# The first two feed-forward tiles of a streaming encoder step by plain products, the seven-product form from the third on

## The chip, the cores and the metric

The kernel runs on one core of a Trainium2 chip. The metric is the time of one launch in microseconds (us) of the device; lower is better. PE is the matrix engine, DVE the vector engine, ACT the scalar engine, POOL the general engine, SP the queue that issues most of the DMAs.

## What is computed

One inference step of a one-layer encoder for 1024 prompt tokens and 8 x 16 sample tokens, 1152 in all, width 1024. The part that matters here is the passage from the first sub-layer to the gated MLP:

```python
x = x + rmsnorm(merged @ p['w_out'], p['g_post1'])
h2 = rmsnorm(x, p['g_pre2'])
...
up = h @ w_ffn_up                      # h = h2: 1152 x 1024 by 1024 x 5632
a, g = jnp.split(up, 2, axis=-1)       # 2816 columns each
ext = jnp.concatenate([buf.astype(a.dtype), a], axis=1)
conv = ext[:, 0:L] * w_dw[0]
for k in range(1, CONV_W):
    conv = conv + ext[:, k:k + L] * w_dw[k]
act = jax.nn.gelu(conv + b_dw) * g
return act @ w_ffn_down
```

## The kernel before

The tokens are held in three chunks of 384 columns (0, 1, 2), features on the partitions in eight blocks of 128. Every matrix product of float32 values is made of three: each operand is split into a high part (ACT copies it to the rounded type, line 63) and a low part (DVE subtracts, line 64), and `mm3` (lines 103, 106, 107) adds hi·hi, hi·lo and lo·hi into one bank of PSUM. Four banks are called `pc`, four `ps`.

`phase_o` multiplies by `w_out`: for chunk c = 0, 1, 2 and output block f = 0 to 7, `out(c, f)` is 24 matmuls of 128x384. ACT copies the bank to `merged[c]` (`mg0`, `mg1`, `mg2` in the traces) and squares it. For each chunk there follow two chains. In the first, `sums` (line 1072) adds the squares over the partitions on PE, `rsqrt` makes the row factors, `row_bcast` (line 96) spreads them over the partitions by one more PE instruction, and `resid` on DVE scales the eight blocks (line 1102), adds x (line 1106; x is loaded and the sum stored to `Dx2` by SP) and accumulates the squares of the result in `ssa` (line 1064). In the second, `sums` and `row_bcast` come again and `norm` (line 1124) scales the rows in place: h2. The chains of chunk c - 1 run beside the products of chunk c; those of chunk 2 run beside the first products of the up GEMM.

The up GEMM works on 22 tiles of ff. Tile ff has two weights of 1024 x 128, one for `a` and one for `g`, which `up_raw` loads into the ring `raw` of three buffers of 512 KB. For chunks 0 and 1 it uses a form with seven products in place of eight: `a` and `g` are the two block rows, the lower and upper four blocks of the inner dimension the two block columns, chunks 0 and 1 the two columns of the right side. The right side's operands are made once: B11, B21 (chunk 0, lower and upper blocks), B22 and T1 to T4 (sums and differences of chunks 0 and 1); those of the left side for each tile by `up_w`: S1 to S4, from the raw weights. Each is split. `up_prod` is one of the seven products: 12 matmuls, then an addition on DVE (or ACT and POOL). Chunk 2 is done by `up_last`, 24 matmuls for `a` and 24 for `g`, with the split weights themselves. `up_act` makes the convolution and the GELU, `up_out` multiplies by `g` and stores.

For tiles 0 and 1 the order is written out at the end of `phase_o`: products 1 and 2 of tile 0, the sums of chunk 2, products 6 and 5, the residual of chunk 2, and so on; the tail of chunk 2 is interleaved. At the start of `phase_u` the weights of these two tiles are loaded and split a second time for chunk 2. From tile 2 on a loop prepares tile ff + 1 while tile ff is multiplied.

The scheduler orders each engine's instructions by a timeline of its own, except where `keep_in_program_order`, `high_priority` or `issue_after` bind it. Each engine, and SP's queue, runs its own list in that order. The pools are rings: `w1` has six tiles of split weights, `w2` four, `m` nine large ones.

Of the kernel before, what the change touches and what calls it, by code (L numbers as in the profile page):

```python
# [10 lines left out]
AF = mybir.ActivationFunctionType  # L11
# [21 lines left out]
class K:  # L33
# [26 lines left out]

    def split(self, hi, lo, src, eng=None):
        nc = self.nc
        nc.scalar.activation(hi, src, AF.Copy)  # L63
        (eng or nc.vector).tensor_sub(lo, src, hi)  # L64

    def load_raw(self, src, shape=(128, 8, 128)):
        r = self.rawtile(list(shape))
# [962 lines left out]
    def phase_o(self):  # L1030
        nc, tc = self.nc, self.tc
        V, G = nc.vector, nc.gpsimd
# [4 lines left out]
        if True:  # L1037
# [75 lines left out]
            def norm(c, rs):  # L1113

                oT = self.merged[c]
                rb = self.row_bcast(P, rs, 3, pin=True)
                if c == 2:
                    self.hhi2 = self.mtile([128, 8, 384], F32R, "h2hi")
                    self.hlo2 = []
                    for tag, n in (("x", 2), ("x", 2), ("ssa", 1), ("ssa", 1), ("sq", 1), ("tmp", 1)):  # L1120
                        t = P.tile([128, n, 384], F32R, tag=tag, name="h2lo")
                        self.hlo2 += [t[:, i] for i in range(n)]
                for f in range(8):
                    V.scalar_tensor_tensor(oT[:, f, :], oT[:, f, :], self.vec[:, V_GPRE2 + f:V_GPRE2 + f + 1], rb,  # L1124
                                           op0=OP.mult, op1=OP.mult)
                    if c == 2:
                        self.split(self.hhi2[:, f, :], self.hlo2[f], oT[:, f, :])

            def op(name, src, eng=None):
                t = self.mtile([128, 2, 4, 384], F32R, "b" + name)  # L1130
# [2 lines left out]

            ss = []
            NF = (0, 5, 4)
            self.B = {}
            lo, up = slice(0, 4), slice(4, 8)
            h0, h1 = self.merged[0], self.merged[1]
            for c in range(3):
                ss.append(ssa())  # L1140
                for f in range(8):
                    self.pin_sq = c == 2
                    if c == 2 and f == 2:
                        self.raws = {0: self.up_raw(0)}
                    out(c, f)
                    if c:
                        if f == 0:
                            rs = sums(ss[c - 1])
                        elif f == 1:
                            with tc.high_priority():  # L1150
                                ss2 = resid(c - 1, rs)
                        elif f == NF[c]:
                            rs = sums(ss2)
                        elif f == NF[c] + 1:
                            with tc.high_priority():
                                norm(c - 1, rs)
                            if c == 1:
                                op("B11", h0[:, lo])
                                op("B21", h0[:, up])
                                V.tensor_sub(h0[:, up], h0[:, up], h0[:, lo])  # L1160
            wms.close()
            self.open_u()
            s0 = self.up_begin(0)
            self.up_w(s0)

            op("B22", h1[:, up])
            V.tensor_sub(h0[:, lo], h1[:, lo], h0[:, lo])
            V.tensor_sub(h1[:, lo], h1[:, up], h1[:, lo])
            V.tensor_sub(h1[:, up], h1[:, up], h0[:, lo])
            op("T2", h1[:, up])  # L1170
            op("T1", h0[:, lo])
            V.tensor_sub(h0[:, up], h0[:, up], h1[:, lo])
            op("T3", h1[:, lo])
            op("T4", h0[:, up])
            self.raws[1] = self.up_raw(1)
            s1 = self.up_begin(1)

            def prods(s, *ps):
                for p in ps:
                    self.up_prod(s, p)  # L1180

            prods(s0, 1, 2)
            rs = sums(ss[2])
            prods(s0, 6, 5)
            with tc.high_priority():
                ss2 = resid(2, rs)
            with tc.issue_after(self.diag.ins):
                self.up_w(s1)
            prods(s0, 7, 3, 4)
            prods(s1, 1, 2)  # L1190
            rs = sums(ss2)
            prods(s1, 6, 5)
            norm(2, rs)
            prods(s1, 7, 3, 4)
            self.first = s0, s1


    def open_u(self):
# [21 lines left out]

    def up_w(self, s, eng=(None,) * 4):

        G = self.nc.vector if s.ff < 2 else self.nc.gpsimd
        ra, rg = self.raws[s.ff]
        a11, a12, a21, a22 = ra[:, 0:4], ra[:, 4:8], rg[:, 0:4], rg[:, 4:8]
        s.aw = self.load_w(None, pool=self.w2, r=ra)
# [11 lines left out]
        s1, s2 = stage()  # L1238
# [15 lines left out]
    def up_prod(self, s, p):  # L1254
# [2 lines left out]
        V = nc.vector  # L1257
        an, bn = {1: ("A11", "B11"), 2: ("A12", "B21"), 6: ("S2", "T2"), 5: ("S1", "T1"), 7: ("S3", "T3"),
                  3: ("S4", "B22"), 4: ("A22", "T4")}[p]
        b = (self.pc() if s.ff < 2 else self.sm())[:, 0:384]  # L1260
        (ah, al), (bh, bl) = s.A[an], self.B[bn]
        for k in range(4):
            self.mm3(b, ah[:, k, :], al[:, k, :], bh[:, k, :], bl[:, k, :], k == 0, k == 3, k == 0)
# [51 lines left out]

    def phase_u(self):
        for s in self.first:

            self.raws[s.ff] = self.up_raw(s.ff)
            s.aw = self.load_w(None, pool=self.w2, r=self.raws[s.ff][0])  # L1320
            self.up_last(s, "a")
            self.up_act(s)
            self.up_wg(s)
            self.up_last(s, "g")
            self.up_out(s)
        cur = None
# [517 lines left out]
```

## Time and profile before

| | us |
|---|---|
| median of 3 runs | 1606.23 (1605.18 to 1611.32) |
| profiled execution | 1607.13 |
| its span in the trace | 1605.3 |
| PE busy | 1546.5 (96%) |
| DVE busy | 1044.1 (65%) |
| ACT busy | 586.4 (37%) |
| mean granted clock of PE | 0.98 |

How to read it: a row of the timeline gives the start in us from the span's start, the time in us, the engine, the line, the operation and its tiles (out<-in), the number of instructions in the row, and in brackets how long the engine was idle before it and what released it. Instructions overlap in the pipe: the starts of a row and of the next give the pace, the durations a little more. A row of the windows gives the length of a stretch, then for each engine its busy time and number of instructions, the granted clock of PE (1.00 is full), the share of the DMA engines and GB/s.

### The profile page before, as it was taken

To read this page: it belongs to the slowest core of one execution; us is meant where nothing else is said; L and a number is where in the kernel's file an instruction comes from. 1 tells how busy PE (TensorE), PEld (TensorE's weight loads), DVE (VectorE), ACT (ScalarE), POOL (GpSimd) and SP (SyncE) were. 2 spreads that over 40 slices of the span, in tenths; PEclk is the share of its full clock that TensorE was granted. 3 is DMA by queue.
4 is the path that set the end of the run, shared out by engine and by line. 5 is a ranking of instruction groups with operands and counts; after the bars stand their busy time and mean duration, and the time that the engine had idled before them with its cause. 6 is when DMAs were issued, how large, how long until landed. Compare 5 with 4: busy or idle time off the path is not lost.

```text
span 1605.3 us, 22914 instructions
## 1 busy us (share of the span) xinstructions
PE 1546.5 (96%) x8964; PEld 1512.9 (94%) x8964; DVE 1044.1 (65%) x1602; ACT 586.4 (37%) x894; POOL 510.8 (32%) x460
## 2 busy tenths in 40 slices
PE   6899999999999999999889999999999999999996
PEld 5899999789899999999879999999999998999996
DVE  7873997655743354637777565656565658788866
ACT  6322544442421242435435433333333333333321
POOL 2400001100021143300016435443443326655546
PEclk9899999999999999999789999999999999999998
DMA  6343333434332235122323211221212143133214
GB/s 247 98 150 96 101 110 107 162 106 117 105 120 81 67 84 164 54 91 91 114 89 138 82 69 66 72 82 69 76 62 82 70 136 137 48 101 105 89 65 167
DMA packets 98460, 163.44 MB, mean 102 GB/s; under 512 B 23216, under 2 KB 68656, under 8 KB 98352
## 3 DMA queue, kind: packets, MB, share of 16 engines
q1 hardware_dynamic: 97920, 161.75, 30.5%
q8 instruction: 70, 1.15, 0.3%
q14 instruction: 38, 0.31, 0.1%
q10 hardware_dynamic: 432, 0.23, 0.0%
HBM read 119.52 MB, written 42.42 MB: 101 GB/s over the span
## 4 chain that ended last, share of the span: by engine, by line
PE 80%; DVE 9%; DMA 3%; issue 2%; ACT 2%; POOL 1%; POOLq 0%; SPq 0%; DVEq 0%; ACTq 0%
PE pc L107 15%; PE pc L103 15%; PE pc L106 14%; PE ps L103 11%; PE ps L106 11%; PE ps L107 11%; DMA Ts<-DG 1%; PE ps L849 1%; DMA DG<-gs 1%; DVE wlo L64 1%; DVE Xs L598 1%; PE ps L1072 1%; DVE mg L1124 1%; PE ps L763 0%; DVE sg L200 0%
## 5 line engine op out<-in xcount | busy, mean ns | idle before, releaser
L103 PE MATMUL pc<-hhi,whi 128*128 128x384 f32 x760 | 259.1, 341 | 7.3 <-ACT hhi L126 7.3
L106 PE MATMUL pc<-hlo,whi 128*128 128x384 f32 x760 | 258.4, 340 | 2.7 <-DVE hlo L127 2.7
L107 PE MATMUL pc<-hhi,wlo 128*128 128x384 f32 x760 | 257.9, 340 | 0.3 <-DVE wlo L64 0.3
L63 ACT ACTIVATE whi<-rawt 128x1024 fp32r<-128x1024 f32 x102 | 107.5, 1055 | 188.6 <-PE pc L106 83.4
L64 DVE TENSOR_TENSOR wlo<-rawt,whi 128x1024 fp32r<-128x1024 f32 x102 | 128.5, 1262 | 56.2 <-ACT whi L63 55.8
L103 PEld LDWEIGHTS pc<-hhi,whi 128*128 128x128 f32 x760 | 144.6, 190 | 9.8 <-ACT hhi L126 7.3
L106 PEld LDWEIGHTS pc<-hlo,whi 128*128 128x128 f32 x760 | 144.2, 190 | 5.4 <-DVE hlo L127 3.6
L107 PEld LDWEIGHTS pc<-hhi,wlo 128*128 128x128 f32 x760 | 144.3, 190 | 2.3 <-issue 0.7
L200 DVE TENSOR_TENSOR sg<-pc,rb 128x384 f32<-128x384 f32 x95 | 52.3, 553 | 117.8 <-PE pc L107 117.4
L107 PE MATMUL pc<-h2hi,wlo 128*128 128x384 f32 x352 | 119.1, 338 | 2.1 <-DVE wlo L64 2.0
L103 PE MATMUL pc<-h2hi,whi 128*128 128x384 f32 x352 | 118.3, 336 | 0.0
L106 PE MATMUL pc<-h2lo,whi 128*128 128x384 f32 x352 | 118.2, 336 | 0.0
L63 ACT ACTIVATE S<-S 128x512 fp32r<-128x512 f32 x88 | 55.3, 630 | 157.9 <-PE ps L107 89.8
L64 DVE TENSOR_TENSOR S<-S,S 128x512 fp32r<-128x512 f32 x88 | 72.5, 826 | 56.2 <-ACT S L63 54.2
L924 ACT ACTIVATE sg<-sg,vec 128x384 f32<-128x384 f32 x72 | 44.1, 613 | 139.0 <-DVE sg L200 108.3
L1011 POOL TENSOR_TENSOR mg<-mg,sgl 128x384 f32<-128x384 f32 x24 | 29.1, 1212 | 165.4 <-DVE sgl L1009 162.0
L103 PE MATMUL ps<-bT,S 128*128 128x384 f32 x240 | 80.2, 334 | 0.0
L107 PE MATMUL ps<-bT,S 128*128 128x384 f32 x240 | 80.2, 334 | 0.0
L106 PE MATMUL ps<-bT,S 128*128 128x384 f32 x240 | 80.2, 334 | 0.0
L63 ACT ACTIVATE dhi<-dwr 128x1024 fp32r<-128x1024 f32 x38 | 39.7, 1058 | 95.2 <-PE pc L106 60.7
L107 PEld LDWEIGHTS pc<-h2hi,wlo 128*128 128x128 f32 x352 | 66.1, 188 | 2.8 <-DVE wlo L64 2.8
L1244 POOL TENSOR_TENSOR S<-rawt 128x512 f32<-128x512 f32 x20 | 27.2, 1361 | 125.6 <-PE ps L107 125.6
(463 smaller groups left out, 4349.7 us busy)
## 6 DMA issues: line engine op xcount, KB each, us to landing
rawt<-in_w_up SPq DMA_DIRECT2D x48, 512.0 KB, 3.4
Dact<-t SPq DMA_DIRECT2D x22, 576.0 KB, 3.5
rawt<-in_w_gate SPq DMA_DIRECT2D x24, 512.0 KB, 3.6
dwr<-in_w_down SPq DMA_DIRECT2D x22, 512.0 KB, 3.4
Dsg<-sg SPq DMA_DIRECT2D x45, 192.0 KB, 1.9
sgl<-Dsg SPq DMA_DIRECT2D x45, 192.0 KB, 2.4
dBr<-Dact SPq DMA_DIRECT2D x8, 768.0 KB, 5.7
xT<-in_xT SPq DMA_DIRECT2D x12, 384.0 KB, 7.6
```

The lines of the kernel that those rows point to most:

```text
L63: nc.scalar.activation(hi, src, AF.Copy)
L64: (eng or nc.vector).tensor_sub(lo, src, hi)
L103: i = nc.tensor.matmul(out, whi, xhi, start=start, stop=False)
L106: nc.tensor.matmul(out, whi, xlo, start=False, stop=False)
L107: nc.tensor.matmul(out, wlo, xhi, start=False, stop=stop)
L200: self.nc.vector.tensor_mul(sg, b, self.rb[:, c, :])
L598: V.tensor_tensor(Xs[64 * i:64 * i + 64, :, g, 1:128], m1[h, :, 0:127], m2[h, :, 0:127], op=op)
L849: nc.tensor.matmul(o, va[:, m, 2 * hp + e, :], pT[:, m, :], start=m == 0, stop=m == 1)
L924: self.nc.scalar.activation(sg, sg, AF.Sigmoid, bias=self.vec[:, V_BGATE + m:V_BGATE + m + 1])
L1011: nc.gpsimd.tensor_add(m, m, sp)
L1072: m = nc.tensor.matmul(s3[:, t:t + 1], s[:, t * 128:t * 128 + 128], self.ones[:, 0:1], start=(i, t) == (0, 0), stop=(i, t) == (len(ss) - 1 ...
L1244: G.tensor_sub(s3, a11, a21)
```

## The change

Tiles 0 and 1 take plain products for all three chunks: for `a` and `g` of each tile 24 matmuls with chunk 0 (B11 and B21), 24 with chunk 1 (a new operand B12, and B22), and 24 with chunk 2 as before. Their weights are loaded once, at `out(2, 2)` and `out(2, 4)`, split at once (`fw`), and kept; S1 to S4 aren't made for them. B12, B22 and T1 are made behind the normalisation of chunk 1; T3, T2 and T4 only behind the normalisation of chunk 2 (`issue_after`). The first use of the seven-product form is tile 2, whose stage operations are now on DVE, not POOL. All seven-form products use the banks `ps`.

```diff
     def split(self, hi, lo, src, eng=None):
-        nc.scalar.activation(hi, src, AF.Copy)
+        a = nc.scalar.activation(hi, src, AF.Copy)
         (eng or nc.vector).tensor_sub(lo, src, hi)
+        return a
...
-                    if c == 2 and f == 2:
-                        self.raws = {0: self.up_raw(0)}
+                    if c == 2 and f in (2, 4):
+                        ff = f // 2 - 1
+                        self.raws[ff] = self.up_raw(ff)
+                        fw.append([self.load_w(None, pool=p, r=r) for p, r in
+                                   zip((self.w1, self.w2 if ff else self.w1), self.raws[ff])])
                     out(c, f)
...
                                 V.tensor_sub(h0[:, up], h0[:, up], h0[:, lo])
+                            else:
+                                op("B12", h1[:, lo])
+                                op("B22", h1[:, up])
+                                V.tensor_sub(h0[:, lo], h1[:, lo], h0[:, lo])
+                                op("T1", h0[:, lo])
...
-            s0 = self.up_begin(0)
-            self.up_w(s0)
-            op("B22", h1[:, up])
...
-            self.raws[1] = self.up_raw(1)
-            s1 = self.up_begin(1)
-            prods(s0, 1, 2)
-            rs = sums(ss[2])
-            prods(s0, 6, 5)
-            with tc.high_priority():
-                ss2 = resid(2, rs)
-            with tc.issue_after(self.diag.ins):
-                self.up_w(s1)
-            prods(s0, 7, 3, 4)
-            prods(s1, 1, 2)
-            rs = sums(ss2)
-            prods(s1, 6, 5)
-            norm(2, rs)
-            prods(s1, 7, 3, 4)
+            first = []
+            for ff in range(2):
+                first.append(self.up_begin(ff))
+                first[ff].aw, first[ff].gw = fw[ff]
+            s0, s1 = self.first = first
+            def plain(s, which, c):
+                w, dst = (s.aw, s.a) if which == "a" else (s.gw, s.g)
+                x = [self.B[n] for n in (("B11", "B21"), ("B12", "B22"))[c]]
+                b = self.proj(w, c, 8, lambda kt, c: x[kt // 4][0][:, kt % 4, :],
+                              lambda kt, c: x[kt // 4][1][:, kt % 4, :], pin=True)
+                nc.scalar.activation(dst[:, self.ch(c)], b, AF.Copy)
+            plain(s0, "a", 0)
+            rs = sums(ss[2])
+            plain(s0, "g", 0)
+            with tc.high_priority():
+                ss2 = resid(2, rs)
+            plain(s1, "a", 0)
+            plain(s1, "g", 0)
+            plain(s0, "a", 1)
+            plain(s0, "g", 1)
+            rs = sums(ss2)
+            plain(s1, "a", 1)
+            with tc.high_priority():
+                last = norm(2, rs)
+            plain(s1, "g", 1)
...
+            with tc.issue_after(last.ins):
+                op("T3", h1[:, lo])
+                op("T2", h1[:, up])
+                op("T4", h0[:, up])
...
@@ up_w
-        G = self.nc.vector if s.ff < 2 else self.nc.gpsimd
+        G = self.nc.vector if s.ff < 3 else self.nc.gpsimd
...
@@ up_prod
-        b = (self.pc() if s.ff < 2 else self.sm())[:, 0:384]
+        b = self.sm()[:, 0:384]
...
@@ phase_u
         for s in self.first:
-            self.raws[s.ff] = self.up_raw(s.ff)
-            s.aw = self.load_w(None, pool=self.w2, r=self.raws[s.ff][0])
             self.up_last(s, "a")
             self.up_act(s)
-            self.up_wg(s)
             self.up_last(s, "g")
             self.up_out(s)
```

How the change moves instructions, at the two places that the prediction speaks of. (In these rows numbers tell tiles of one name apart, and "waits" lists the engines and DMA channels on which an instruction waits.)

Place A: DVE, the end of the residual of chunk 1, whose last addition to `ssa_6983` the sums on PE wait for. Before; rawt_7032 and rawt_7034 are the weights of tile 0, loaded long before:

```order
L1106 TENSOR_TENSOR mg1_4081<-mg1_4081,x_7008 128x384 [waits DMAHW3_49,DVE_49]
L64 TENSOR_TENSOR S4_7272<-S_7266,S4_7272 128x512 [waits Activation_49]
L1106 TENSOR_TENSOR mg1_4081<-mg1_4081,x_7008 128x384 [waits DVE_49]
L1064 TENSOR_TENSOR ssa_6983<-ssa_6983,sq_6992 128x384 [waits Activation_49]
L64 TENSOR_TENSOR wlo_7254<-rawt_7032,whi_7253 128x1024 [waits PE_49,Activation_49]
L1064 TENSOR_TENSOR ssa_6983<-ssa_6983,sq_7002 128x384 [waits DVE_49,Activation_49]
L1106 TENSOR_TENSOR mg1_4081<-mg1_4081,x_7021 128x384 [waits DMAHW6_49]
L1106 TENSOR_TENSOR mg1_4081<-mg1_4081,x_7021 128x384
L1064 TENSOR_TENSOR ssa_6983<-ssa_6983,sq_7005 128x384 [waits DVE_49,Activation_49]
L64 TENSOR_TENSOR wlo_7276<-rawt_7034,whi_7275 128x1024 [waits PE_49,Activation_49]
L1064 TENSOR_TENSOR ssa_6983<-ssa_6983,sq_7015 128x384 [waits DVE_49]
L1064 TENSOR_TENSOR ssa_6983<-ssa_6983,sq_7018 128x384 [waits DVE_49]
```
After; rawt_7102 and rawt_7104 are the weights of tile 1, rawt_7748 the first of tile 2:

```order
L1107 TENSOR_TENSOR mg1_4081<-mg1_4081,x_7008 128x384 [waits DMAHW3_49,DVE_49]
L1107 TENSOR_TENSOR mg1_4081<-mg1_4081,x_7008 128x384 [waits DVE_49]
L64 TENSOR_TENSOR wlo_7107<-rawt_7102,whi_7106 128x1024 [waits DMAHW5_49,PE_49,Activation_49]
L1065 TENSOR_TENSOR ssa_6983<-ssa_6983,sq_6992 128x384 [waits Activation_49]
L64 TENSOR_TENSOR wlo_7111<-rawt_7104,whi_7110 128x1024 [waits DMAHW6_49,PE_49,Activation_49]
L1107 TENSOR_TENSOR mg1_4081<-mg1_4081,x_7021 128x384 [waits DMAHW0_49,DVE_49]
L1107 TENSOR_TENSOR mg1_4081<-mg1_4081,x_7021 128x384 [waits DVE_49]
L1065 TENSOR_TENSOR ssa_6983<-ssa_6983,sq_7002 128x384 [waits DVE_49]
L1065 TENSOR_TENSOR ssa_6983<-ssa_6983,sq_7005 128x384 [waits DVE_49]
L1065 TENSOR_TENSOR ssa_6983<-ssa_6983,sq_7015 128x384 [waits DVE_49,Activation_49]
L64 TENSOR_TENSOR wlo_7755<-rawt_7748,whi_7754 128x1024 [waits DMAHW2_49,PE_49,Activation_49]
L1065 TENSOR_TENSOR ssa_6983<-ssa_6983,sq_7018 128x384 [waits DVE_49]
```
The stage operations S1 to S4 of tile 0 stood ahead of and between these rows and are gone; three splits of weights now stand in the chain, two of them of tile 1.

SP at the same place. Before:

```order
L1108 DMA Dx2_6238<-mg1_4081 128x2x384 [waits DMAHW5_49,DVE_49]
L1101 DMA x_7021<-in_xT 128x768 [waits DMAHW1_49]
L1108 DMA Dx2_6238<-mg1_4081 128x2x384 [waits DMAHW7_49,DVE_49]
L68 DMA rawt_7298<-in_w_up 128x1024 [waits DMAHW0_49]
L1101 DMA x_7380<-in_xT 128x768 [waits DMAHW3_49,DVE_49]
L1108 DMA Dx2_6238<-mg1_4081 128x2x384 [waits DMAHW2_49]
L68 DMA rawt_7300<-in_w_up 128x1024 [waits DVE_49]
```
After; x_6995, which rawt_7102 follows in the ring `raw`, is read by two additions of the residual just ahead of those on x_7008:

```order
L69 DMA rawt_7102<-in_w_up 128x1024 [waits DMAHW5_49,DVE_49]
L69 DMA rawt_7104<-in_w_up 128x1024 [waits DMAHW0_49,DVE_49]
L1109 DMA Dx2_6238<-mg1_4081 128x2x384 [waits DMAHW7_49,DVE_49]
L1102 DMA x_7021<-in_xT 128x768 [waits DMAHW1_49]
L1109 DMA Dx2_6238<-mg1_4081 128x2x384 [waits DVE_49]
L69 DMA rawt_7748<-in_w_up 128x1024 [waits DMAHW2_49]
```
The two loads of tile 1 moved ahead of the stores of chunk 1 and of the load of x_7021.

Place B: DVE, the residual of chunk 2 (mg2), whose last addition the next sums wait for. Before:

```order
L1244 TENSOR_TENSOR S_7441<-rawt_7298,rawt_7300 128x512
L1245 TENSOR_TENSOR S_7441<-rawt_7298,S_7432 128x512
L1102 SCALAR_TENSOR_TENSOR mg2_4082<-mg2_4082,vec_72,ps_7377 128x384 [waits PE_49]
L1102 SCALAR_TENSOR_TENSOR mg2_4082<-mg2_4082,vec_72,ps_7377 128x384
L64 TENSOR_TENSOR S3_7444<-S_7441,S3_7444 128x512 [waits Activation_49]
L1106 TENSOR_TENSOR mg2_4082<-mg2_4082,x_7380 128x384 [waits DMAHW1_49,DVE_49]
L64 TENSOR_TENSOR S4_7447<-S_7441,S4_7447 128x512 [waits Activation_49]
L1106 TENSOR_TENSOR mg2_4082<-mg2_4082,x_7380 128x384 [waits DVE_49]
L1284 TENSOR_TENSOR ax_7251<-v_7371,pc_7471 128x384 [waits PE_49]
L1064 TENSOR_TENSOR ssa_7379<-ssa_7379,sq_7388 128x384 [waits Activation_49]
L1102 SCALAR_TENSOR_TENSOR mg2_4082<-mg2_4082,vec_72,ps_7377 128x384 x2
L64 TENSOR_TENSOR wlo_7451<-rawt_7300,whi_7450 128x1024 [waits PE_49,Activation_49]
```
After:

```order
L1103 SCALAR_TENSOR_TENSOR mg2_4082<-mg2_4082,vec_72,ps_7352 128x384 [waits PE_49]
L1103 SCALAR_TENSOR_TENSOR mg2_4082<-mg2_4082,vec_72,ps_7352 128x384
L1107 TENSOR_TENSOR mg2_4082<-mg2_4082,x_7355 128x384 [waits DMAHW3_49,DVE_49]
L1107 TENSOR_TENSOR mg2_4082<-mg2_4082,x_7355 128x384 [waits DVE_49]
L1065 TENSOR_TENSOR ssa_7354<-ssa_7354,sq_7363 128x384 [waits Activation_49]
L1103 SCALAR_TENSOR_TENSOR mg2_4082<-mg2_4082,vec_72,ps_7352 128x384 x2
L1107 TENSOR_TENSOR mg2_4082<-mg2_4082,x_7366 128x384 [waits DMAHW7_49,DVE_49]
L1107 TENSOR_TENSOR mg2_4082<-mg2_4082,x_7366 128x384 [waits DVE_49]
L1065 TENSOR_TENSOR ssa_7354<-ssa_7354,sq_7373 128x384 [waits Activation_49]
L1065 TENSOR_TENSOR ssa_7354<-ssa_7354,sq_7376 128x384 [waits DVE_49,Activation_49]
```
The splits of S3, S4 and of a weight, and the addition after a product, no longer stand between the residual's operations.

More of the change, by code (lines that the diff above doesn't have):

```diff
@@ L1126, in norm @@
                     if c == 2:
-                        self.split(self.hhi2[:, f, :], self.hlo2[f], oT[:, f, :])
+                        a = self.split(self.hhi2[:, f, :], self.hlo2[f], oT[:, f, :])
+                return a if c == 2 else None
             def op(name, src, eng=None):
@@ L1135, in phase_o @@
             NF = (0, 5, 4)
-            self.B = {}
+            self.B, self.raws, fw = {}, {}, []
             lo, up = slice(0, 4), slice(4, 8)
@@ L1167, in phase_o @@
-            V.tensor_sub(h0[:, lo], h1[:, lo], h0[:, lo])
+            first = []
[9 more added lines that the diff above has]
+                nc.scalar.activation(dst[:, self.ch(c)], b, AF.Copy)
@@ L1169, in phase_o @@
             V.tensor_sub(h1[:, up], h1[:, up], h0[:, lo])
-            op("T2", h1[:, up])
-            op("T1", h0[:, lo])
             V.tensor_sub(h0[:, up], h0[:, up], h1[:, lo])
-            op("T3", h1[:, lo])
-            op("T4", h0[:, up])
-            self.raws[1] = self.up_raw(1)
-            s1 = self.up_begin(1)
-            def prods(s, *ps):
-                for p in ps:
-                    self.up_prod(s, p)
-            prods(s0, 1, 2)
-            rs = sums(ss[2])
-            prods(s0, 6, 5)
@@ L1185, in phase_o @@
-            with tc.high_priority():
-                ss2 = resid(2, rs)
-            with tc.issue_after(self.diag.ins):
-                self.up_w(s1)
-            prods(s0, 7, 3, 4)
-            prods(s1, 1, 2)
-            rs = sums(ss2)
-            prods(s1, 6, 5)
-            norm(2, rs)
-            prods(s1, 7, 3, 4)
-            self.first = s0, s1
+            with tc.issue_after(last.ins):
+                op("T3", h1[:, lo])
+                op("T2", h1[:, up])
+                op("T4", h0[:, up])
```

## The prediction

> **What bounds the kernel now.** I read the page first, then the windows of 10 us, the waits of PE, and last the timeline of PE, DVE, ACT and the DMA issues around the place that is edited.
>
> ```profile
> PE 1546.5 (96%) x8964; PEld 1512.9 (94%) x8964; DVE 1044.1 (65%) x1602; ACT 586.4 (37%) x894; POOL 510.8 (32%) x460
> ```
>
> ```profile
> core 0: us, PE busy (x) PEld busy (x) DVE busy (x) ACT busy (x) POOL busy (x), PEclk, DMA share, GB/s
> ...
> 760.00:770.00 10.00, 6.18 (x35) 5.89 (x34) 9.70 (x18) 7.33 (x14) 0.00 (x0) 0.88 0.87 294
> ...
> 790.00:800.00 10.00, 8.16 (x40) 7.90 (x40) 9.27 (x7) 6.41 (x9) 1.71 (x1) 0.75 0.14 49
> ...
> 810.00:820.00 10.00, 3.97 (x23) 3.65 (x22) 8.80 (x16) 4.09 (x7) 0.00 (x0) 0.94 0.69 234
> 820.00:830.00 10.00, 8.77 (x35) 8.71 (x36) 4.10 (x8) 3.02 (x8) 2.77 (x3) 0.54 0.19 70
> ...
> 850.00:860.00 10.00, 7.99 (x46) 7.67 (x45) 9.08 (x7) 7.07 (x10) 8.44 (x8) 1.00 0.42 146
> ...
> 900.00:950.00 50.00, 50.00 (x289) 50.00 (x288) 31.00 (x32) 18.12 (x26) 22.30 (x22) 1.00 0.19 66
> ```
>
> The program is bound by PE. In the steady part 289 products take 50 us, so one 128x384 product costs 0.173 us. The stretch 760 to 860 is the exception: PE has holes, DVE is full, and behind each hole the granted clock is below 1. The holes have names:
>
> ```profile
> PE ps L1072 <- DVE ssa L1064: 10.9, 3, 6.6
> PE pc L107 <- DVE wlo L64: 2.0, 1, 2.0
> PE pc L106 <- DVE bT L64: 1.8, 1, 1.8
> ```
>
> ```profile
> 746.69 0.80 PE L1072 MATMUL ps<-ones,ssa 128*128 128x1 f32 x6 [0.43 <-DVE ssa L1064]
> ...
> 768.74 1.41 PE L1072 MATMUL ps<-ones,ssa 128*128 128x1 f32 x6 [3.82 <-DVE ssa L1064]
> ...
> 772.56 0.67 PE L103 MATMUL pc<-mhi,whi 128*128 128x384 f32 x1
> ...
> 779.29 0.81 PE L96 MATMUL ps<-diag,ones 128*128 128x384 f32 x2
> ...
> 788.25 0.33 PE L103 MATMUL pc<-bB,whi 128*128 128x384 f32 x1
> ...
> 792.42 0.72 PE L1072 MATMUL ps<-ones,ssa 128*128 128x1 f32 x6
> ...
> 793.73 0.44 PE L103 MATMUL pc<-bT,S 128*128 128x384 f32 x1
> ...
> 796.01 0.69 PE L106 MATMUL pc<-bT,S 128*128 128x384 f32 x1 [1.84 <-DVE bT L64]
> ...
> 820.60 1.41 PE L1072 MATMUL ps<-ones,ssa 128*128 128x1 f32 x6 [6.63 <-DVE ssa L1064]
> ...
> 861.81 0.34 PE L103 MATMUL ps<-bB,whi 128*128 128x384 f32 x1
> ```
>
> PE's order is the same in both kernels up to 788.25, the first product of tile 0 (DVE's differs from 746.69 on), and again from 861.81 on, the first of the seven products of the third tile. Behind that PE is busy 50.00 of 50.00 us. So the whole effect is the shift of that one product. The first wait (3.82 us, place A) is for the sums after the residual of chunk 1; the second is for T2 in the seven-product form; the third (6.63 us, place B) is for the sums after the residual of chunk 2; the fourth (2.0 us) is for the weights of tile 0, loaded and split again.
>
> From 788.25 to 861.81 PE issues 14x12 + 4x24 + 24 = 288 products, 49.9 us at 0.173, in 73.6 us. So 23.7 us there are waits, sums, row broadcasts and half-clock time.
>
> **The change, part by part.** Added: eight plain products of 24 in place of fourteen of 12, that is 192 for 168, 24 more, 4.2 us of PE at full clock, all on the path. B12 is one more split of 128x1536, counted below.
>
> Removed: for tiles 0 and 1 the eight stage operations and eight splits of S1 to S4, four loads of 512 KB and their reload splits, and the evacuations by DVE (ACT copies the plain products instead, at the 0.47 of its other evacuations). That DVE work stands before the waits at A and B now; at B the order shows nothing of it left, at A something worse is put in its place.
>
> Place A. The rows that I price it with:
>
> ```profile
> 753.51 0.68 DVE L64 TENSOR_TENSOR S<-S,S 128x512 fp32r<-128x512 f32 x1
> 754.12 4.28 DVE L1102 SCALAR_TENSOR_TENSOR mg<-mg,vec,ps 128x384 f32<-128x384 f32 x8
> ...
> 759.86 1.95 DVE L1106 TENSOR_TENSOR mg<-mg,x 128x384 f32<-128x384 f32 x4
> ...
> 763.27 1.21 DVE L64 TENSOR_TENSOR wlo<-rawt,whi 128x1024 fp32r<-128x1024 f32 x1
> ```
>
> ```profile
> 760.87 1.05 ACT L63 ACTIVATE whi<-rawt 128x1024 fp32r<-128x1024 f32 x1
> 761.82 0.47 ACT L1085 ACTIVATE mg<-pc 128x384 f32<-128x384 f32 x1
> 762.19 1.75 ACT L1060 ACTIVATE sq<-mg 128x384 f32<-128x384 f32 x4
> ```
>
> For the loads of weights, from issue to landing, two answers: one load issued at 806.63 with nothing ahead of it, and the three issued from 761.94 to 767.55 behind stores and loads of 384 KB.
>
> ```profile
> DMA to landing us min/median/max: 3.3/3.3/3.3
> DMA to landing us min/median/max: 6.7/7.5/8.0
> ```
>
> In the new order DVE splits four weights between the residual's operations, and the first of tile 1 (wlo_7107) needs a load that takes the ring's buffer of x_6995: it is issued only behind the two additions that read x_6995. DVE runs in its order, so the additions of squares behind that split wait too. Worked out: without the S work DVE may start the eight multiplications at 752.8 (the broadcast, not DVE, is then last); 4.2 to 757.0; the split of 1.15 to 758.2; five operations of 0.47 to 760.5. The load is issued there, lands after 3.4 at 764.0, and ACT splits it in 1.05 to 765.1. ACT then has two evacuations of 0.37 and four squares of 0.44 ahead of the second weight: 767.6, and 768.7 with its split. DVE: 1.15 to 769.8, five operations of 0.47 to 772.2, the third split to 773.4, the last addition to 773.9. The sums start at 773.9 instead of 768.74: **5.2 us later**. The nearest rows for a landing are 3.3 (nothing ahead) and 8.0 (a full queue). I take 3.4, since nothing but the stores of chunk 0 was issued before it. The split waiting on ACT holds back the evacuation of out(2, 2); PE has a free bank for each product up to its sums, where it waits anyhow. On SP the two loads pass three stores, which nobody awaits, and x_7021, which even at 8.0 from about 762 is there when DVE asks at 769.8. At 8.0 the sums start at 778.5; with the load there at once, ACT's row of work still gives 770.7.
>
> Between A and the first plain product nothing changes: 788.25 becomes 793.4. The product takes 24 x 0.173, to 797.6.
>
> The sums of chunk 2 come next. Their last addition now stands behind five operations of 128x1536:
>
> ```profile
> 784.81 1.75 DVE L1167 TENSOR_TENSOR mg<-mg,mg 128x1536 f32<-128x1536 f32 x1
> 786.48 1.75 DVE L64 TENSOR_TENSOR bB<-mg,bB 128x1536 fp32r<-128x1536 f32 x1
> ...
> 832.09 4.29 DVE L1124 SCALAR_TENSOR_TENSOR mg<-mg,vec,ps 128x384 f32<-128x384 f32 x8
> ```
>
> The normalisation of chunk 1 starts 1.0 behind the broadcast of 779.29 + 5.2, at 785.3; 4.2 for its eight rows, 0.5 for an addition, 5 x 1.67 (the two starts above) and 0.5: 798.8. PE waits **1.2 us** there.
>
> Then 1.3 for the sums (792.42 to 793.73), seven plain products, 29.1, two row broadcasts of at most 0.8, and 2.0 for the sums of three columns at place B: 832.8. Place B itself costs nothing: the residual of chunk 2 is 8 x 0.53 + 8 x 0.47 + 5 x 0.47 = 10.4 on DVE with about 2 of waits for squares, from 805.1 to 818, and PE comes to its sums at 821. Three microseconds are the cover; if they are gone the sums wait.
>
> The last normalisation starts one plain product (4.15) before the end of that stretch, plus 0.4, at 829.1, and its eight rows end at 833.3. The first low half of chunk 2 is there at 833.8, and PE could use it at 832.9: **0.9** of waiting. Then five products of 24, 20.8, without reloads: **854.5**.
>
> ```profile
> 846.76 1.42 DVE L1309 SCALAR_TENSOR_TENSOR t<-ax,vec,t 128x1152 f32<-128x1152 f32 x1
> ```
>
> T3, T2, T4 and S1 to S4 of the third tile come into these 20.8 us on DVE: eight low halves of 0.47, three T of 1.67, four stage operations and four splits of 0.61 (753.51 to 754.12), and two steps of the convolution of 1.4, 16.5 in all from 833.3, so to 850 with no wait. PE asks for the first of them, T2 and S2, two products of 12 behind 854.5, at 858.7: some 9 us of cover, behind which the third tile's products would wait.
>
> Sum: 854.5 against 861.81 is 7.3 us less. The profiled execution lasted 1607.13 (span 1605.3), 0.9 above the median of the runs, 1606.23; so 1599.8 for such an execution and 1598.9 for the median. I say 1599. By parts: 24 products +4.2, place A +5.2, and all waits and half-clock time behind 788.25 together -16.7.
>
> **The clock.** The windows show that it falls to half behind a hole. At half clock a product costs 0.32:
>
> ```profile
> 773.55 0.32 PE pc L107
> 773.87 0.32 PE pc L103
> ```
>
> At 793.73 it fell when sums of 1.3 us and a hole of 2.1 came together (0.75 in that window); at 857 a hole of 2.3 between products did not do it (1.00). The new wait of 1.2 with its 1.3 of sums is 2.5 together, between the two, nearer to the one that cost nothing, so I take nothing. If it falls as at 793.73, for the time to the next broadcast, some 19 products pay 0.147 each: 2.8 us.
>
> [...]
>
> **The rivals.** First, place A is not longer than the load forces: the load of tile 1 is already on its way or lands at once, and the sums start at 770.7. That is 3.2 less than my sum, 1595.7 for the median. For it speaks that DVE has 5.6 us of S work less there; against it that the load waits for x_6995.
>
> Second, the loads are slow and the gain is used up: a landing of 8.0 adds 4.6 (1603.5), or the clock falls at the wait of 1.2 us (1601.7). For it speak the DMA share of 0.87 in 760 to 770 and the row at 793.73. Both together are 1606.3, no change at all.
>
> Third, slower than before: the clock stays at half in the plain products. The hole at A grows from 4 to 9 us, and PE would have to stay at half behind it. Each product there pays 0.147; from 50 products on (7.3 / 0.147) the gain is gone, and with all 192 the time is 1598.9 + 28.2 = 1627. Against it: behind 772.56 the clock was back within 24 products, also behind the hole of 6.63 us.
>
> **How the numbers follow.** My forecast 0.50, with its own range of 1596.5 to 1601.5 (2.5 us either way, the spread of landings between 3.3 and 6.7 and of the clock's windows); the first rival 0.20, the second 0.20, the third and other losses 0.10. A measurement of this kernel can tell about 0.5%, 8 us, from no change: 1598.2 is the bound. Of the forecast's 0.50 about 0.20 lies under it, and the first rival is under it: faster 0.40. The rest of the forecast and the second rival: same 0.50. Slower 0.10. The range goes from 2.5 under the first rival to the second one's 1606: 1593 to 1606.
>
> **What would show it.** In the profile after, the wait of the sums after chunk 1's residual is 8 to 10 us and its releaser stands behind a wlo of a weight of w_up; the sums of chunk 2 wait about 1 us, those at place B not at all; no wait for wlo of reloaded weights; the first seven-form product near 854. It is wrong if the sums at A start before 770 or behind 779, if PE waits at B (then DVE's residual took over 16 us), or if the third tile's second or third product waits for T2 or S2.

## The result and the profile after

The changed kernel takes 1595.49 us in the median (1593.05 to 1599.88) beside 1606.23 of the kernel before (1605.15 to 1611.32, both timed in turn on one chip): a ratio of 0.9931, with a 95% interval of 0.9911 to 0.9951. That is 0.7% faster, just past the 0.5% that I took as the least that can be told. The forecast of 1599 us was 3.5 us too high, and the time lies under its own range (1596.5 to 1601.5) and inside the whole one (1593 to 1606); the first rival had given 1595.7.

The profiled execution lasted 1594.72 us, its span is 1592.9, 12.4 less than before. The windows and the waits of PE after:

```profile
core 0: us, PE busy (x) PEld busy (x) DVE busy (x) ACT busy (x) POOL busy (x), PEclk, DMA share, GB/s
760.00:770.00 10.00, 4.58 (x25) 4.29 (x25) 7.75 (x13) 5.39 (x10) 0.00 (x0) 0.80 0.95 352
...
790.00:800.00 10.00, 8.73 (x53) 8.17 (x52) 6.77 (x7) 2.15 (x6) 2.08 (x1) 1.00 0.06 20
...
820.00:830.00 10.00, 9.49 (x53) 8.90 (x52) 7.15 (x15) 6.44 (x12) 0.00 (x0) 1.00 0.00 0
...
900.00:950.00 50.00, 50.00 (x289) 50.00 (x288) 29.98 (x32) 18.02 (x25) 20.59 (x21) 1.00 0.19 67
```

```profile
engine line waited for: us in total, times, longest us
PE ps L1073 <- DVE ssa L1065: 7.1, 3, 5.4
PE pc L107 <- DVE h2lo L64: 0.5, 1, 0.5
```

From 780 to 950 the clock is 1.00 in every window; the waits for T2 (1.8) and for a reloaded weight (2.0) are gone, and of the waits for `ssa` the one at A grew from 3.8 to 5.4, the one of 6.6 is gone and one of 1.3 is new. The steady part is as before, 289 products in 50 us. PE in order of time:

```profile
744.90 0.80 PE L1073 MATMUL ps<-ones,ssa 128*128 128x1 f32 x6 [0.43 <-DVE ssa L1065]
...
768.53 1.41 PE L1073 MATMUL ps<-ones,ssa 128*128 128x1 f32 x6 [5.42 <-DVE ssa L1065]
...
772.37 0.67 PE L104 MATMUL pc<-mhi,whi 128*128 128x384 f32 x1
...
778.38 0.81 PE L97 MATMUL ps<-diag,ones 128*128 128x384 f32 x2
...
787.35 0.33 PE L104 MATMUL pc<-bB,whi 128*128 128x384 f32 x1
...
792.94 0.80 PE L1073 MATMUL ps<-ones,ssa 128*128 128x1 f32 x6 [1.27 <-DVE ssa L1065]
...
794.27 0.42 PE L104 MATMUL pc<-bB,whi 128*128 128x384 f32 x1
...
815.81 0.72 PE L1073 MATMUL ps<-ones,ssa 128*128 128x1 f32 x6
...
826.81 0.34 PE L104 MATMUL pc<-h2hi,whi 128*128 128x384 f32 x1
827.66 0.45 PE L107 MATMUL pc<-h2lo,whi 128*128 128x384 f32 x1 [0.51 <-DVE h2lo L64]
...
848.58 0.34 PE L104 MATMUL ps<-bB,whi 128*128 128x384 f32 x1
```

The sums at 744.90 (746.69 before) are the last instruction that both kernels reach alike; I count from there ("the common sums") to the first of the third tile's seven products, and call this the stretch. Before it is 861.81 - 746.69 = 115.12 us, after 848.58 - 744.90 = 103.68: 11.4 less. The other 1.0 of the span's 12.4 lies outside: the common sums come 1.8 earlier and the part behind the stretch is 0.8 longer (743.5 and 744.3), without any difference in PE's instructions there.

### The profile page after: what moved, and what is told of

The parts are those of the page before. It is cut to its first block, busy times and chain, and to the rows that moved or that the text cites. A ratio compares the mean times of both kernels' runs of the same rounds, so it can differ in the third digit from the quotient of the medians.

```text
span 1592.9 us, 22896 instructions
## 1 busy us (share of the span) xinstructions
PE 1542.2 (97%) x8988; PEld 1509.1 (95%) x8988; DVE 1023.7 (64%) x1577; ACT 582.0 (37%) x887; POOL 500.8 (31%) x452
## 3 DMA queue, kind: packets, MB, share of 16 engines
q8 instruction: 70, 1.15, 0.3%
## 4 chain that ended last, share of the span: by engine, by line
PE 82%; DVE 8%; DMA 4%; issue 2%; ACT 1%; POOL 0%; POOLq 0%; SPq 0%; DVEq 0%; ACTq 0%
PE pc L108 15%; PE pc L107 15%; PE pc L104 15%; PE ps L104 11%; PE ps L107 11%; PE ps L108 11%; DMA Ts<-DG 1%; PE ps L850 1%; DVE mg L1125 1%; DMA DG<-gs 1%; DMA qr<-Dq 1%; PE ps L1073 1%; DVE wlo L64 1%; DVE Xs L599 1%; DVE sg L201 0%
## 5 line engine op out<-in xcount | busy, mean ns | idle before, releaser
L63 ACT ACTIVATE whi<-rawt 128x1024 fp32r<-128x1024 f32 x98 | 103.3, 1055 | 190.3 <-PE pc L107 91.6
L64 DVE TENSOR_TENSOR wlo<-rawt,whi 128x1024 fp32r<-128x1024 f32 x98 | 123.4, 1261 | 56.0 <-ACT whi L63 55.6
L63 ACT ACTIVATE S<-S 128x512 fp32r<-128x512 f32 x80 | 50.3, 630 | 149.2 <-PE ps L108 88.9
L64 DVE TENSOR_TENSOR S<-S,S 128x512 fp32r<-128x512 f32 x80 | 66.5, 835 | 49.8 <-ACT S L63 47.6
L107 PEld LDWEIGHTS pc<-h2lo,whi 128*128 128x128 f32 x352 | 65.9, 187 | 0.8 <-DVE h2lo L64 0.8
L104 PE MATMUL pc<-mhi,whi 128*128 128x384 f32 x192 | 66.5, 346 | 0.0
```

The lines of the kernel that those rows point to most:

```text
L63: a = nc.scalar.activation(hi, src, AF.Copy)
L104: i = nc.tensor.matmul(out, whi, xhi, start=start, stop=False)
L107: nc.tensor.matmul(out, whi, xlo, start=False, stop=False)
```

## The experiments

In all of them the stretch is read from one profiled execution, and the ratio from timed runs beside runs of the kernel before on the same chip.

| kernel | stretch, us | median, us | ratio to before (95%) |
|---|---|---|---|
| before | 115.12 | 1606.23 | 1 |
| changed kernel | 103.68 | 1595.49 | 0.9931 (0.9911 to 0.9951) |
| before, stage work on POOL | 114.09 | 1604.76 | 0.9995 (0.9982 to 1.0008) |
| before, sums later | 110.20 | 1601.15 | 0.9968 (0.9956 to 0.998) |
| changed, weight of tile 1 behind the chain | 97.42 | 1589.90 | 0.9908 (0.9884 to 0.9932) |
| changed, sums later | 97.71 | 1588.28 | 0.9896 (0.9877 to 0.9916) |
| changed, both of these | 93.76 | 1583.64 | 0.9861 (0.9842 to 0.988) |
| changed, that weight late in the chain | 109.84 | 1599.72 | 0.9963 (0.995 to 0.9977) |
| changed, reload | 106.07 | 1595.51 | 0.9943 (0.9921 to 0.9966) |
| changed, 24 products more | 107.25 | 1597.72 | 0.9956 (0.9942 to 0.997) |
| changed, sums at B two products earlier | 109.63 | 1601.79 | 0.997 (0.9954 to 0.9986) |

**Is the gain the stage work that leaves DVE?** In the kernel before, the stage operations of tiles 0 and 1 go to POOL:

```diff
-        G = self.nc.vector if s.ff < 2 else self.nc.gpsimd
+        G = self.nc.gpsimd
```

> The kernel before with the stage additions for S1 to S4 of tiles 0 and 1 on POOL in place of DVE (2.4 us of DVE less at each of the places A and B); products, reloads and splits as before. Theory 1: this relieves DVE by part of what the change takes from it: the hole at A shrinks by about 2 us, the one at B by 1 to 2, T2 and the reload's wait stay: 1602 to 1604. Rival: the whole gain of the change was the stage work on DVE, not the plain products; then near 1597.

It gave 1.0 us of the stretch and nothing that the timed runs tell from the kernel before. The hole at A is 0.4 us shorter and not 2, the one at B 1.5; T2 and the reload are waited for as before, and the 1602 to 1604 of the theory are missed. The stretch also has 3.4 us less of half clock than that of the kernel before (23.9 and 27.3), so even the 1.0 is not the stage work's for certain. The rival is out as far as these operations go: the eight splits of S1 to S4 stay on DVE here, and no run moves them alone.

**Is the gain in the sums that come too early?** In the kernel before, the sums after chunk 1's residual come one product later:

```diff
-            NF = (0, 5, 4)
+            NF = (0, 5, 5)
```

> The kernel before with only the sums of chunk 1's residual one product later. Theory 1, refined by the seven-form's own need: the hole at A (4 us) goes, but the third of the seven products needs T2, which comes out of the same chain about 4 us earlier than now, so PE waits there some 6 us instead of 2: of the 8 us (hole and half clock) about 4 stay, 1602. Rival: each hole stands alone, and 8 us are gained, 1598.

```profile
engine line waited for: us in total, times, longest us
PE pc L103 <- ACT bT L63: 5.1, 1, 5.1
PE ps L1072 <- DVE ssa L1064: 4.7, 2, 4.2
PE pc L107 <- DVE wlo L64: 2.0, 1, 2.0
PE pc L106 <- DVE bT L64: 1.7, 1, 1.7
```

The hole at A is gone, but 6.8 us of waits for T2 stand in its place, since T2 needs chunk 1's h2. What the theory said of T2 came true; the time still fell by 0.3%, and the stretch by 4.9 us. So in the seven-product form moving the sums mostly moves the wait: all of PE's waits from the common sums on (their own 0.4 included) add up to 14.3 us here and to 15.3 before. The rest of the 4.9 goes with the clock, which is at half for 20.5 us instead of 27.3.

**What is left at place A in the changed kernel?** A copy of one column into the load's buffer makes tile 1's first load wait for the first four additions of x (it is issued at 759.81, behind the copy at 758.72); the scheduler then puts the three weight splits behind the last addition that the sums need:

```diff
-                        self.raws[ff] = self.up_raw(ff)
+                        self.raws[ff] = self.up_raw(ff, h1[:, 3, 0:1] if ff else None)
...
+        if behind is not None:
+            r = self.rawtile([128, 8, 128])
+            self.nc.vector.tensor_copy(r[:, 0, 0:1], behind)
+            self.nc.sync.dma_start(r, self.I["w_up"][ff])
+            return [r, self.load_raw(self.I["w_up"][ff + NFF])]
```

> The changed kernel, with the first weight of tile 1 loaded only behind the first additions of x in the residual of chunk 1 (one copy of one column, 128x1, forces it); the scheduler then puts the three splits of weights behind the last addition of squares instead of between. Theory 1: the hole at place A (5.75 us from the last product to the sums in the changed kernel) is made by those three splits and their loads in DVE's list. Then the sums start as soon as PE comes to them, the hole is under 1 us, the clock stays full there, and the first seven-form product comes 8 to 10 us earlier: 1586 to 1588. Rival: the hole is the residual's own length (its 8 multiplications, 8 additions, 5 additions of squares, and the load of x); then it stays at 4 us or more and the time within 2 us of 1595.

```profile
763.23 0.80 PE L1073 MATMUL ps<-ones,ssa 128*128 128x1 f32 x6 [1.15 <-DVE ssa L1065]
...
841.28 0.34 PE L104 MATMUL ps<-bB,whi 128*128 128x384 f32 x1
```

The wait fell from 5.42 to 1.15, so the rival is out: three splits of 1.15 and the 0.93 that DVE waited at one of them are 4.4 us, most of the hole. The theory promised too much all the same: the hole is 1.5 us and not under 1, the clock still fell behind it (3.4 us at half), the stretch is 6.3 us shorter and not 8 to 10, and the median is 2 us over the 1588 expected.

**The other way to the same end**: the sums at A and those of chunk 2 one product later, with the residual of chunk 2 behind them:

```diff
-            NF = (0, 5, 4)
+            NF = (0, 5, 5)
...
             plain(s0, "a", 0)
-            rs = sums(ss[2])
             plain(s0, "g", 0)
+            rs = sums(ss[2])
+            plain(s1, "a", 0)
             with tc.high_priority():
                 ss2 = resid(2, rs)
-            plain(s1, "a", 0)
```

> The changed kernel with PE's order altered alone: the sums of chunk 1's residual one product of 24 later (behind out(2,5)), the sums and the broadcast of chunk 2 one plain product later. DVE's work is the same. Theory 1 (the holes are waits of PE for DVE's chain, and each is filled by products that don't need it): the hole at A falls from 5.75 to about 1.5 us, the one at the sums of chunk 2 (1.6) goes, the clock does not fall; the first seven-form product 8 to 10 us earlier, 1586 to 1588. Rival: the chain on DVE is the bound of this stretch, so that what is filled at one place is waited for at the next; then under 3 us, 1593 or more.

```profile
769.84 0.80 PE L1073 MATMUL ps<-ones,ssa 128*128 128x1 f32 x6 [1.33 <-DVE ssa L1065]
770.50 2.63 PE L1073 MATMUL ps<-ones,sq 128*128 128x1 f32 x12
```

The wait is 1.33, the clock falls at the sums (2.63 us for the twelve, 1.48 at full clock in the next kernel) and stays at half for 6.8 us, against the theory, and no wait is left at the sums of chunk 2. The stretch is 6.0 us shorter where 8 to 10 were expected. **Both edits together:**

> Both earlier edits of the changed kernel together: tile 1's first weight is loaded only behind the first additions of x, so that its split leaves the chain of chunk 1's residual, and the sums of chunk 1's residual and of chunk 2 each come one product later. Theory (each hole is the distance between the end of the DVE chain and PE's arrival at the sums, so one more product of 4.2 us in front of each removes what is left): hole at place A under 0.3 us, none at the sums of chunk 2, no stretch of half clock behind A; from the common sums to the first seven-form product 95 to 96.5 us (97.4 and 97.7 with one of the edits, 103.7 with none), 1585 to 1588 us. Rival (what is left in each of the two is the clock or another chain that comes up in its place): no better than the better of the two, 97.4 or more and 1588 to 1590.

```profile
engine line waited for: us in total, times, longest us
PE ps L97 <- ACT diag L95: 0.5, 1, 0.5
PE pc L107 <- DVE h2lo L64: 0.5, 1, 0.5
PE ps L1073 <- DVE ssa L1065: 0.4, 1, 0.4
```

```profile
760.00:770.00 10.00, 10.00 (x66) 10.00 (x65) 6.43 (x10) 6.32 (x12) 0.52 (x1) 1.00 0.89 333
```

The 0.4 for `ssa` is at the common sums; nothing is waited for at A, the clock stays at 1.00, and the stretch is 93.76, even under the forecast. This version beats both kernels: 1583.64 us, 1.4% under the kernel before.

**Was only the time of that load wrong in the prediction?** Here the load is made late, as the prediction had it, and DVE's order is bound so that the splits stay in the chain (the residual of chunk 1 is written in two parts, and the second is bound to the program's order together with the splits; the rest of the edit loads tile 0's weights as before and carries these arguments):

```diff
-                        self.raws[ff] = self.up_raw(ff)
-                        fw.append([self.load_w(None, pool=p, r=r) for p, r in
-                                   zip((self.w1, self.w2 if ff else self.w1), self.raws[ff])])
...
+                        self.raws[1] = self.up_raw(1, h1[:, 3, 0:1])
...
+                        def load(g):
+                            if g == 5:
+                                for p, r in zip((self.w1, self.w2), self.raws[1]):
+                                    fw[1].append(self.load_w(None, pool=p, r=r, pin=True))
+                        with tc.high_priority():
+                            self.pin_sq = True
+                            ss2 = resid(1, None, range(4, 8), st1, load)[1]
```

> The changed kernel with what the prediction assumed at place A: the load of tile 1's first weight is issued only behind the two additions that read x_6995 (a copy of one column into its buffer makes it wait), and DVE's order is bound so that the two splits of tile 1 and one of tile 2 stand between the additions of squares that the sums wait for. Theory (the prediction's working of place A was right, and only the time of that load was wrong): the load is issued some 15 us behind the common sums, lands 3.4 later, and with ACT's and DVE's splits and the additions behind them the sums of chunk 1's residual start 27 to 28.5 us behind the common sums (23.6 in the changed kernel, 22.1 in the kernel before, 27.2 by the prediction); the hole is 9 to 10.5 us and the first seven-form product 107 to 109 us behind the common sums, 1598 to 1601 us. Rival (a late load costs little, since DVE's splits and squares fill the time): sums by 24.5 us, no more than 1 us over the changed kernel.

SP, DVE and PE (the common sums stand at 744.55 here; the line numbers are a few higher):

```profile
759.15 0.72 SPq L1255 DMA_DIRECT2D rawt<-in_w_up  x1
...
766.10 2.36 DVE L80 TENSOR_TENSOR wlo<-rawt,whi 128x1024 fp32r<-128x1024 f32 x2 [4.60 <-ACT whi L79]
...
770.68 1.41 PE L1077 MATMUL ps<-ones,ssa 128*128 128x1 f32 x6 [7.91 <-DVE ssa L1069]
```

The load is issued 14.6 us behind the common sums, DVE stands for 4.6 us at its split, and the sums start 26.1 behind the common sums, a little under the 27 to 28.5 expected, 2.5 later than in the changed kernel and not the 1 that the rival allowed. The hole is 8.2 us, under the 9 to 10.5 expected; in DVE's order here the additions of x_7021 come last, which the prediction had in between. The stretch is 6.2 longer: 2.9 up to the first plain product, and 3.2 behind it, where the clock fell at the sums of chunk 2 and stayed at half for 6.8 us (last section); with that fall it is 0.8 over the 107 to 109 expected.

**The other terms**, three edits of the changed kernel: the reload of the weights of tiles 0 and 1 put back, one plain product of 24 done twice, and the sums at place B two plain products earlier.

```diff
         for s in self.first:
+            self.raws[s.ff] = self.up_raw(s.ff)
+            s.aw = self.load_w(None, pool=self.w2, r=self.raws[s.ff][0])
             self.up_last(s, "a")
             self.up_act(s)
+            s.gw = self.load_w(None, pool=self.w2, r=self.raws[s.ff][1])
```

> The changed kernel with the weights of tiles 0 and 1 loaded and split a second time at the start of the last products of chunk 2, as the kernel before does. Theory: the reload's splits come back between the low halves of chunk 2 on DVE and PE waits for one of them as before (2.0 us there): 2 to 3 us more from the common sums to the first seven-form product, 105.5 to 107 us instead of 103.7, 1597 to 1598.5 us. Rival (the splits fit into DVE's free time there): within 0.5 us of 103.7.

```profile
PE ps L1073 <- DVE ssa L1065: 7.5, 3, 5.8
PE pc L108 <- DVE wlo L64: 1.1, 1, 1.1
PE pc L107 <- DVE h2lo L64: 1.1, 2, 0.5
```

A wait for the reloaded weight (1.1) and one more for a low half come back, and the stretch is 2.4 longer, as expected (2.2 of it behind the first plain product); the median of the timed runs (1595.51, with 1597 to 1598.5 expected) doesn't show it, so its price rests on the trace alone.

```diff
             plain(s0, "a", 1)
+            plain(s0, "a", 1)
             plain(s0, "g", 1)
```

> The changed kernel with one of its plain products (24 matmuls, tile 0, a, chunk 1) done twice. It prices the term for the 24 products that the plain form has more. Theory (PE is the bound there, all at full clock): 4.15 us more, 107.8 us from the common sums to the first seven-form product, or 0.5 less where the wait for the first low half of chunk 2 goes away. Rival (DVE's chain is the bound at place B, so the product fills a gap): under 1 us more.

```profile
787.78 0.33 PE L104 MATMUL pc<-bB,whi 128*128 128x384 f32 x1
...
853.21 0.34 PE L104 MATMUL ps<-bB,whi 128*128 128x384 f32 x1
```

From the first plain product to the first seven-form product 65.43 us, beside 61.23 in the changed kernel: 4.2 for 24 products, the term of the prediction.

```diff
-            plain(s0, "a", 1)
-            plain(s0, "g", 1)
             rs = sums(ss2)
-            plain(s1, "a", 1)
+            plain(s0, "a", 1)
             with tc.high_priority():
                 last = norm(2, rs)
+            plain(s0, "g", 1)
+            plain(s1, "a", 1)
             plain(s1, "g", 1)
```

> The changed kernel with the sums after chunk 2's residual (place B) two plain products earlier, behind two and not four since the residual was ordered; the products that are passed come behind the sums. It measures the cover of place B. Theory (DVE ends the residual 4.0 us before PE reaches the sums): PE comes 8.3 us earlier, waits 4.3 us for the last addition, and the wait of 0.5 for the low half goes away: 3.8 us more, 107.5 us, up to 2 more if the clock drops behind the hole. Rival (PE would have time to spare there, since the broadcast or the residual itself goes faster): hole under 2 us.

```profile
810.56 0.87 PE L1073 MATMUL ps<-ones,ssa 128*128 128x1 f32 x6 [2.34 <-DVE ssa L1065]
812.60 0.59 PE L1073 MATMUL ps<-ones,sq 128*128 128x1 f32 x2 [1.17 <-ACT sq L1061]
```

PE is done with its last product at 808.05 and gets the last of the chain, squares from ACT, at 812.60: 4.5 us, where 4.3 were forecast, so the chain of chunk 2's residual ends about four microseconds ahead of need in the changed kernel. The clock fell behind this hole too (products 0.32 us apart up to 817.9), and the stretch is 6.0 longer, the upper end of what was expected.

## Why the prediction was right and where it was off

The steps, counted from the common sums of each kernel:

| step | before | forecast | after |
|---|---|---|---|
| sums after chunk 1's residual (A) | 22.05 | 27.2 | 23.63 |
| first plain product | 41.56 | 46.7 | 42.45 |
| first seven-form product | 115.12 | 107.8 | 103.68 |

By kind, the 11.4 us are these: PE's waits fell from 15.3 us to 7.6, the 24 products more cost 4.2, and 7.9 us are left. That fits the clock, which was at half for 27.3 us of the stretch before and for 10.2 after: an estimate, at 0.173 us a product and not 0.32, is 7.8 us at most for these 17.1.

**The step that failed is place A**, forecast at 5.2 us later, measured 1.6. The prediction had named the sign for it: the sums at A started before 770 (at 768.53), after a wait of 5.4 us and not of 8 to 10. It said that the first weight of tile 1 "takes the ring's buffer of x_6995" and "is issued only behind the two additions that read x_6995". SP and DVE after:

```profile
747.59 8.86 SPq L69 DMA_DIRECT2D rawt<-in_w_up  x2
...
758.89 0.59 SPq L69 DMA_DIRECT2D rawt<-in_w_up  x1
```

```profile
746.35 1.21 DVE L64 TENSOR_TENSOR wlo<-rawt,whi 128x1024 fp32r<-128x1024 f32 x1
...
757.42 1.96 DVE L1107 TENSOR_TENSOR mg<-mg,x 128x384 f32<-128x384 f32 x4
759.29 1.22 DVE L64 TENSOR_TENSOR wlo<-rawt,whi 128x1024 fp32r<-128x1024 f32 x1
...
763.01 1.03 DVE L1107 TENSOR_TENSOR mg<-mg,x 128x384 f32<-128x384 f32 x2 [0.90 <-DMA x<-in_xT]
...
766.69 1.23 DVE L64 TENSOR_TENSOR wlo<-rawt,whi 128x1024 fp32r<-128x1024 f32 x1 [0.93 <-ACT whi L63]
```

The first load of tile 1 is issued at 747.59, the moment that the low half of tile 0's first weight (746.35 and 1.21) is done: it took that weight's buffer, landed 3.1 us later, and its split at 759.29 waits for nothing. (The second load of that row went out at 756.1, behind the low half of tile 0's second weight.) The buffer of x_6995 went to the first weight of tile 2, issued at 758.89 behind the additions at 757.42. The buffers of this ring didn't come in the order that I assumed in the section on the change and in the prediction. What remained of the wait at the head of DVE's list is small: DVE waits 0.93 at the split of tile 2's weight, which took 6.7 us to land, and 0.90 for x_7021, which I had called harmless. The late-load kernel shows the mechanism itself: with the load as the prediction had it, the sums come 26.1 us behind the common sums, where it had 27.2. And the order could have told: with the load late, the scheduler by itself put the splits behind the chain (the kernel with the weight behind the chain). That it left the first split ahead of the additions, in the rows shown under the change, could have been read as a sign that it took this load to be early.

**0.7 us more came from the clock at A.** From the sums to the broadcast it took 10.55 before and 9.85 after, with the same instructions: the half clock ended 9.2 us behind the sums before (at 777.90) and 7.7 after (at 776.22). It lasted 10.24 us in both; only its place against the sums differs, and that is the place of the clock's grid in these two executions (last section). So the 0.7 is luck and not the change.

**Everything behind the first plain product came as worked out**: 61.23 us, by the prediction 854.5 - 793.4 = 61.1. In it the hole at the sums of chunk 2 is 1.6 with a wait of 1.27 (forecast 1.2), none is at place B, the low half is waited for 0.51 (0.9), and 20.9 us of products follow (20.8). One part of this is luck: that the clock didn't fall at the sums of chunk 2 hung on where the hole lay, and not on its length, by which the prediction had reasoned; with the same hole of 2.8 us the kernel with the late load lost 3.2 us there (last section). The prediction's range of 2.5 us either way counts in the clock's windows, for which it has no length from a row; what the runs showed is half clock in stretches of 3.41 us or a multiple of it. The rows of DVE for place B and for the third tile's operands:

```profile
799.37 1.14 DVE L1103 SCALAR_TENSOR_TENSOR mg<-mg,vec,ps 128x384 f32<-128x384 f32 x2 [3.23 <-PE ps L97]
...
810.81 1.02 DVE L1107 TENSOR_TENSOR mg<-mg,x 128x384 f32<-128x384 f32 x2
...
822.85 4.29 DVE L1125 SCALAR_TENSOR_TENSOR mg<-mg,vec,ps 128x384 f32<-128x384 f32 x8 [11.02 <-PE ps L97]
...
841.59 2.49 DVE L64 TENSOR_TENSOR S<-S,S 128x512 fp32r<-128x512 f32 x4
```

DVE's last operation of the residual ends at 811.8, 4 us ahead of PE's sums (cover forecast: 3), and the splits that T2 and S2's product needs end by 844.1, 8.6 us before PE asks at 848.58 + 4.16 (forecast: 9). The sum: -7.3 forecast, -3.6 at A, -0.7 of clock, and 0.1 the other way make, but for rounding, the measured -11.4.

**The first rival**, the load already under way, is what came, at 1.6 instead of 2.0 later. The second and third didn't: the one slow load (6.7 us) held DVE up for 0.93, and the clock didn't stay low. The chance of 0.20 for the first rival was too little: what I held against it, that the load waits for x_6995, rested on the order of a ring that no row of the profile had shown.

## What to carry to other kernels

Work that stands between an engine's row of operations and another engine's wait costs by the time at which its own input comes (here the sums at A came 23.6 us behind the common sums with the load issued at 2.7, and 26.1 with it issued at 14.6); before it is priced, settle from the trace which buffer its load gets and when that falls free. An order that a scheduler made can be evidence itself: here it placed the split early when the load was early, and late when the load was made late. When PE waits for a chain, look for work that can be put in front of the consumer (one product more) and for work that can leave the chain: here each alone left a wait of 1.2 or 1.3 us and a fall of the clock, and the two together neither.

## What the runs showed of the hardware

In the eleven profiled executions, between 735 and 862 us, half clock came in stretches of 3.41 us or a multiple of it (6.83, 10.24, 13.65), and in one execution they lay on one grid: in the kernel before they began at 767.66, 794.97 and 818.86, 8 and 7 times 3.41 apart. In the whole spans of the kernel before and the changed kernel it was so too, but for the stretch that the end of each cuts off. The grid's place differed from one execution to the next. The windows below are cut on that grid: the kernel before, the changed kernel, and the kernel with the late load, all at the sums of chunk 2 (length; busy PE, weight loads, DVE, ACT, POOL; clock; DMA).

```profile
791.56:794.97 3.41, 2.62 (x19) 2.35 (x18) 3.41 (x4) 2.78 (x3) 0.00 (x0) 1.00 0.01 4
794.97:798.38 3.41, 2.37 (x7) 2.37 (x8) 3.41 (x3) 1.52 (x4) 1.71 (x1) 0.50 0.02 5
```

```profile
789.87:793.28 3.41, 2.14 (x15) 1.85 (x13) 3.41 (x4) 0.49 (x1) 0.00 (x0) 1.00 0.18 69
793.28:796.70 3.42, 3.42 (x25) 3.42 (x25) 2.86 (x2) 0.17 (x1) 1.93 (x1) 1.00 0.02 5
```

```profile
792.99:796.40 3.41, 2.14 (x16) 1.85 (x15) 3.41 (x4) 0.49 (x1) 0.00 (x0) 1.00 0.07 24
796.40:799.81 3.41, 3.41 (x14) 3.41 (x14) 2.33 (x2) 0.51 (x3) 1.65 (x1) 0.50 0.02 5
```

PE's busy time, which has the one-column sums in it, doesn't tell these apart: with 2.62 in the first pair and 2.14 in the third the clock fell, and with 2.14 in the second it stayed. Counted by what lies between 128x384 products (from the timelines, each product taken as 0.173 us at full clock and 0.32 at half), the first windows of the three pairs have 2.38, 1.79 and 2.30 us without one. In the eleven profiled executions, between 735 and 862 us, every window at full clock with 2.24 us or more without products (17 of them) was followed by half clock, and none with 2.02 or less; at half clock, the full clock came back after windows with 0.76 or less, and not after 0.80 or more. So the same hole of 2.8 us (products apart, at full clock) cost nothing in the changed kernel, where the grid cut it in two, and 3.2 us in the kernel with the late load. It stands in six of the executions, and the clock fell behind it in this one alone. That corrects the prediction's words on the row at 793.73: sums of 1.3 and a hole of 1.1 lay in one window there. Whether the grid's place is also behind the 1 us outside the stretch and the spread of the timed runs stays open: ahead of the common sums the clock was at half for 17.07 us in the kernel before and for 13.65 in the changed kernel, and two executions don't settle it.
